# Group B's recurrence in a two-layer decoder trunk: own and neighbour products made elementwise and summed by a ones matmul

## The chip, the cores and the metric

The kernel runs on one core of one Trainium2 chip. The metric is the device time of one execution in microseconds (us), the median of several runs. The engines are TensorE (PE; PEld is its weight load), VectorE (DVE), ScalarE (ACT), GpSimd (POOL) and SyncE (SP), which here issues most of the DMAs.

## What is computed

A trunk of one even and one odd layer over x of 512 tokens by 2048. The even layer has a normalisation, one input projection, two groups of heads (A: windowed attention, B: a gated linear recurrence), gates and an output projection. The odd layer has stick-breaking attention. The change is in group B, which the reference computes for 8 heads of 128 in chunks:

```python
def hgrn2_chunkwise(q, logf, k, v):
    ...
    pair = jnp.exp(jnp.minimum(bcum[:, :, :, :, None, :] - bcum[:, :, :, None, :, :], 0.0))
    att = jnp.einsum('bhnik,bhnjk,bhnijk->bhnij', qc, kc, pair)
    att = jnp.where(causal, att, 0.0)
    o_intra = jnp.einsum('bhnij,bhnjv->bhniv', att, vc)
    ...
    o_inter = jnp.einsum('bhnik,bhnkv->bhniv', qc * jnp.exp(bcum), s_prev)
    o = o_intra + o_inter
```

Here q is SiLU of one projection (bq), k and the forget factor f come from another (bf), v from a third (bi), and a fourth (bg) gives the output gate. Token i sees token j (j not after i) by the sum over the 128 channels of q_i, k_j and the product of the forget factors between them.

## The kernel before

**Projections.** Every tile has 128 partitions by 512 columns (channels by tokens, or a block of 128 tokens by 512 channels). Values of float32 are carried as two exact parts, `hi` on ScalarE (L154) and `lo` on VectorE (L155), both made by `split`. `proj_t` makes 128 output channels for all 512 tokens: 16 pieces of the contraction with three 128x512 matmuls each. `proj_n` makes 512 channels by token blocks. Weights come in chunks through SP (L171) into three raw buffers, are split into three hi and three lo buffers, and `take` keeps the work three chunks ahead. A chunk of `proj_t` holds 8 of the 16 pieces.

**Interleaving.** A head's own work is a generator. After every second piece of a projection (6 matmuls) `tick` runs it up to its next `yield`; the number yielded is how many ticks are left out then. So TensorE's order is written by the program: six or more matmuls of a projection, then one step of a head. `later` queues a generator behind at most one other. The other engines' order is set when the program is built, from the order of the code, its priorities (`urgent`) and its dependences, and each engine runs its own list in order.

**Group B.** For each of the 8 heads the loop at the end of the printed code runs `forget(proj_t)` (bf), `decays`, `gate(proj_t)` for q (L266 to L273: VectorE, ScalarE, VectorE), qd = q times f (L688), `gate(proj_t)` for the output gate, and then queues `attn_b`, whose steps run inside the next head's projections. In head 7, before qd, four tiles of y, the heads' outputs that lie in DRAM (`ydr`), are read back (`load_y`, L297) and split, for the output projection that follows.

**attn_b.** It builds the 128x128 blocks of attention between k and q, transposed, in the tile at0. `blocks` makes four float32 matmuls, one for each token block. The first group uses the bare q and is multiplied by the identity (L610): a token with itself. Then come seven levels: level lv takes runs of 2^lv tokens, and pairs each second run's q with the first run's k. Levels 0 to 4 use `blocks` over the whole block and copy the masked places into at0 (copy_predicated, L636); levels 5 and 6 use small matmuls and ScalarE copies (L627). Every level scales q and k in place by factors of the decay (L631, L633). Blocks that lie further apart go into at1 (L641) and at2 (L650, on ScalarE). The o step then multiplies at0, at1 and at2 with v into one bank, squares the result, splits the square (`x_`), sums it over channels with a matmul against the all-ones tile `onr`, and writes y (L675 to `keep_y`, L290). at0, at1 and at2 are tiles of pool x (19 buffers); q, k and the parts of y are in pool u (62); banks of PSUM for the heads are the 4 of pool pa.

Also met by the prediction: L482 is GpSimd's product in group A's attention, L372 its products in the rotary step, L495 transposes on TensorE.

Of the kernel before, what the change touches and what calls it, by code (L numbers as in the profile page):

```python
# [10 lines left out]
F32R = mybir.dt.float32r  # L11
# [3 lines left out]
ALU = mybir.AluOpType  # L15
# [4 lines left out]
P = 128  # L20
D = 2048
S = 512
NC = D // P
NB = S // P
# [67 lines left out]
def trunk(ctx, tc, xt, w, lnT, lbT, gnT, qkn, sink, cs, amask, bmask, eye, cmask, out):  # L92
# [29 lines left out]
    def bank(pool):  # L122
        cnt[0] += 1
        return pool.tile([P, S], F32, tag="b", name=f"b{cnt[0]}")
# [59 lines left out]
    def proj_t(rhs, c_first=0, c_last=NC - 1):  # L184
        ps = bank(pp)
        c = c_first - 1
        while c < c_last:
            hi, lo, c0, n, wd = take()
            for ci in range(n):
                c = c0 + ci  # L190
                a, b = hi[:, ci * P:(ci + 1) * P], lo[:, ci * P:(ci + 1) * P]
                mm(ps, a, rhs[c][0], c == c_first, False)
                mm(ps, a, rhs[c][1], False, False)
                mm(ps, b, rhs[c][0], False, c == c_last)
                if c % 2:
                    tick()
        return ps
# [64 lines left out]
    def gate(ps, bc):  # L262

        g = U()
        with urgent():
            V.tensor_tensor(out=g, in0=ps, in1=bc, op=ALU.mult)  # L266
        t = U()
        A.activation(out=t, in_=g, func=AF.Abs)
        A.activation(out=t, in_=t, func=AF.Exp, scale=-1.0)
        A.activation(out=t, in_=t, func=AF.Ln, bias=1.0)  # L270
        V.scalar_tensor_tensor(out=t, in0=g, scalar=0.0, in1=t, op0=ALU.min, op1=ALU.subtract)
        A.activation(out=t, in_=t, func=AF.Exp)
        V.tensor_tensor(out=g, in0=g, in1=t, op=ALU.mult)  # L273
        return g
# [313 lines left out]
            V.tensor_tensor(out=res[-1], in0=d[:, :, 0], in1=d[:, :, 1], op=ALU.mult)  # L588
        return res

    def attn_b(hd, decs, k, q, qd, g, v):
        dec = decs[7]
        vc = slice((hd % 4) * P, (hd % 4) * P + P)
        at0 = X()
        at1 = X()
        at2 = X()
        b = bank(pa)

        def blocks(b, q):
            for t in range(NB):  # L600
                s = slice(t * P, (t + 1) * P)
                mm(b[:, s], k[:, s], q[:, s], t == 0, True)

        def halves(x, ln_):
            return x.rearrange("p (n z l) -> p n z l", z=2, l=ln_)

        blocks(b, q)
        q = qd
        v4 = lambda x: x.rearrange("p (b q) -> p b q", b=NB)
        V.tensor_tensor(out=v4(at0), in0=v4(b), in1=ident.unsqueeze(1).to_broadcast([P, NB, P]), op=ALU.mult)  # L610
        yield 2
        for lv in range(7):
            ln_ = 1 << lv
            b = bank(pa)
            if lv < 5:
                blocks(b, q)
            else:
                nw = 64 // ln_
                win = b[:ln_, :NB * 64].rearrange("p (b w q) -> p b w q", b=NB, w=nw)
                for t in range(NB):  # L620
                    for w_ in range(nw):
                        c0 = t * P + 2 * ln_ * w_
                        mm(win[:, t, w_], k[:, c0:c0 + ln_], q[:, c0 + ln_:c0 + 2 * ln_], t + w_ == 0, True)
                a4 = v4(at0)
                for w_ in range(nw):
                    r0 = 2 * ln_ * w_
                    A.activation(out=a4[r0:r0 + ln_, :, r0 + ln_:r0 + 2 * ln_], in_=win[:, :, w_], func=AF.Copy)  # L627
            n = S // (2 * ln_)
            d = decs[lv][:, :2 * n].rearrange("p (n z) -> p n z", z=2)
            qh, kh = halves(q, ln_), halves(k, ln_)  # L630
            V.tensor_tensor(out=qh[:, :, 1], in0=qh[:, :, 1],  # L631
                            in1=d[:, :, 0:1].to_broadcast([P, n, ln_]), op=ALU.mult)
            V.tensor_tensor(out=kh[:, :, 0], in0=kh[:, :, 0],  # L633
                            in1=d[:, :, 1:2].to_broadcast([P, n, ln_]), op=ALU.mult)
            if lv < 5:
                V.copy_predicated(out=v4(at0), mask=bm[lv].unsqueeze(1).to_broadcast([P, NB, P]), data=v4(b))  # L636
            yield 1
        b = bank(pa)
        for i, t in enumerate((1, 3)):
            mm(b[:, i * P:(i + 1) * P], k[:, (t - 1) * P:t * P], q[:, t * P:(t + 1) * P], i == 0, True)  # L640
        A.activation(out=at1[:, :2 * P], in_=b[:, :2 * P], func=AF.Copy)  # L641
        for t in (1, 3):
            qs, ks = q[:, t * P:(t + 1) * P], k[:, (t - 1) * P:t * P]
            V.tensor_scalar(out=qs, in0=qs, scalar1=dec[:, t - 1:t], scalar2=None, op0=ALU.mult)
            V.tensor_scalar(out=ks, in0=ks, scalar1=dec[:, t:t + 1], scalar2=None, op0=ALU.mult)
        yield 1
        b = bank(pa)
        for t in range(2):
            mm(b[:, t * 2 * P:(t + 1) * 2 * P], k[:, t * P:(t + 1) * P], q[:, 2 * P:], t == 0, True)
        A.activation(out=at2, in_=b, func=AF.Copy)  # L650
        yield 1
        o = bank(pa)
        vt = [v[t][:, vc] for t in range(NB)]
        for t in range(NB):
            s = slice(t * P, (t + 1) * P)
            mm(o[:, s], vt[t], at0[:, s], t == 0, False)
        for i, t in enumerate((1, 3)):
            mm(o[:, t * P:(t + 1) * P], vt[t - 1], at1[:, i * P:(i + 1) * P], False, False)
        for t in range(2):
            mm(o[:, 2 * P:], vt[t], at2[:, t * 2 * P:(t + 1) * 2 * P], False, t == 1)  # L660
        sq = X()
        A.activation(out=sq, in_=o, func=AF.Square)
        sh = X(F32R)
        sl = X(F32R)
        split(sq, sh, sl)
        yield 2
        b = bank(pa)
        mm(b, onr, sh, True, False)
        mm(b, onr, sl, False, True)
        vv = X()  # L670
        A.activation(out=vv, in_=b, func=AF.Identity, scale=1.0 / P, bias=epst)
        r = X()
        rsqrt(vv, r, sq)
        y = X()
        V.scalar_tensor_tensor(out=y, in0=o, scalar=gn, in1=r, op0=ALU.mult, op1=ALU.mult)  # L675
        V.tensor_tensor(out=y, in0=y, in1=g, op=ALU.mult)
        keep_y(8 + hd, y)

    for grp in range(2):
        v = evac_nat(proj_n(h, pp, 512), nat0, 512)  # L680
        for hd in range(4 * grp, 4 * grp + 4):
            f, k = forget(proj_t(h), hd)
            decs = decays(f)
            q = gate(proj_t(h), bc0)
            if hd == B_HEADS - 1:
                yy = [load_y(c) for c in range(4)]
            qd = U()
            V.tensor_tensor(out=qd, in0=q, in1=f, op=ALU.mult)  # L688
            g = gate(proj_t(h), bc0)
            later(attn_b(hd, decs, k, q, qd, g, v))  # L690


    def out_proj(cut, resid, finish, yy):
# [232 lines left out]
```

## Time and profile before

| | |
|---|---|
| median of 3 runs | 1831.55 us (1831.22 to 1833.01) |
| profiled execution | 1832.02 us |
| its span | 1830.2 us |
| busy in the span | TensorE 1815.9, its weight loads 1517.9, VectorE 1006.9, ScalarE 775.0, GpSimd 113.2 us |
| DMA | 193.50 MB, mean 106 GB/s |
| stretch of group B's heads | about 363 to 735 us |

The span runs from the first to the last instruction of the profile; the execution's own time has 1.8 us around it. Busy times are those of an engine's instructions; matmuls are pipelined, so one matmul row is longer (0.39 us) than the distance from its start to the next one's. For what a matmul costs, starts are compared.

### The profile page before, as it was taken

The page shows a single profiled execution, that of the slowest core. Times are in us where ns is not written, and L with a number is a line of the kernel's source. Part 1 is how long each engine was busy: PE and PEld are TensorE (multiplying, and loading weights), DVE is VectorE, ACT ScalarE, POOL GpSimd, SP SyncE. Part 2 cuts the span into 40 slices and gives each one's busy share as a digit, 9 for nine tenths or more (in the row PEclk, how much of TensorE's full clock was granted, in tenths as well). Part 3 has the DMA queues.
Part 4 walks back from the last instruction along what each step waited for, and adds up shares of the span by engine and source line. Part 5 has one row for each costly group of instructions (what it writes and reads, how often), then busy time and mean ns, then how long its engine had stood idle before and what let it go on. Part 6 is the DMA issues. An engine that isn't in the chain of part 4 may idle for free.

```text
span 1830.2 us, 22453 instructions
## 1 busy us (share of the span) xinstructions
PE 1815.9 (99%) x8788; PEld 1517.9 (83%) x8788; DVE 1006.9 (55%) x1519; ACT 775.0 (42%) x1285; POOL 113.2 (6%) x96
## 2 busy tenths in 40 slices
PE   8999999999999999999999999999999999999999
PEld 6978888888888888888888888888888888888887
DVE  7486777866456666444435552565355634556334
ACT  6454646544343444334334432544244434444211
POOL 4112212200000000013000000000000000000000
PEclk9999999999999999999999999999999999999999
DMA  6222232222222226334222222222222222235424
GB/s 229 93 83 81 93 104 81 92 81 75 76 86 87 75 98 210 125 137 144 100 92 98 87 92 102 89 87 96 92 89 94 85 99 93 97 115 183 152 81 155
DMA packets 66633, 193.50 MB, mean 106 GB/s; under 512 B 7904, under 2 KB 8416, under 8 KB 66528
## 3 DMA queue, kind: packets, MB, share of 16 engines
q1 hardware_dynamic: 64224, 187.88, 30.2%
q10 hardware_dynamic: 2304, 4.20, 0.7%
q8 instruction: 69, 1.13, 0.2%
q14 instruction: 36, 0.29, 0.0%
HBM read 175.27 MB, written 16.78 MB: 105 GB/s over the span
## 4 chain that ended last, share of the span: by engine, by line
PE 86%; POOL 0%; issue 0%; DVE 0%
PE b L151 85%; PE b L802 1%; PE b L495 0%; POOL x L372 0%; PE b L426 0%; DVE lo L155 0%; DVE u L724 0%; PE b L409 0%; DVE u L374 0%
## 5 line engine op out<-in xcount | busy, mean ns | idle before, releaser
L151 PE MATMUL b<-u,hi 128*128 128x512 f32 x3584 | 1119.8, 394 | 0.0
L151 PEld LDWEIGHTS b<-u,hi 128*128 128x128 f32 x3584 | 663.6, 188 | 131.8
L151 PE MATMUL b<-u,lo 128*128 128x512 f32 x1792 | 699.3, 390 | 0.6 <-DVE lo L155 0.6
L154 ACT ACTIVATE hi<-raw 128x1024 fp32r<-128x1024 f32 (+2 forms) x307 | 312.4, 1018 | 791.9 <-PE b L151 727.0
L155 DVE TENSOR_TENSOR lo<-raw,hi 128x1024 fp32r<-128x1024 f32 (+2 forms) x307 | 363.2, 1184 | 360.8 <-ACT hi L154 353.4
L151 PEld LDWEIGHTS b<-u,lo 128*128 128x128 f32 x1792 | 336.5, 188 | 72.1 <-DVE lo L155 1.0
L151 PE MATMUL b<-hi,u 128*128 128x512 f32 (+1 forms) x1152 | 344.8, 383 | 9.3 <-ACT u L321 6.2
L151 PEld LDWEIGHTS b<-hi,u 128*128 128x128 f32 x1152 | 211.4, 190 | 49.4 <-ACT u L321 6.2
L151 PE MATMUL b<-lo,u 128*128 128x512 f32 (+1 forms) x576 | 218.8, 380 | 0.8 <-DVE lo L155 0.8
L151 PEld LDWEIGHTS b<-u,u 128*128 128x128 f32 (+2 forms) x928 | 115.7, 176 | 14.9 <-issue 3.5
L151 PEld LDWEIGHTS b<-lo,u 128*128 128x128 f32 x576 | 109.2, 190 | 21.5 <-DVE lo L155 1.2
L151 PE MATMUL b<-u,u 128*128 128x128 f32 (+5 forms) x928 | 126.8, 281 | 0.0
L282 POOL TENSOR_TENSOR u<-u,u 128x512 f32<-128x512 f32 x30 | 52.5, 1751 | 523.6 <-ACT u L281 523.0
L266 DVE TENSOR_TENSOR u<-b,bc 128x512 f32<-128x512 f32 x40 | 27.5, 689 | 80.0 <-PE b L151 79.8
L151 PE MATMUL b<-x,u 128*128 128x128 f32 (+3 forms) x360 | 65.4, 327 | 0.0
L155 DVE TENSOR_TENSOR x<-x,x 128x512 fp32r<-128x512 f32 (+2 forms) x56 | 32.4, 578 | 58.4 <-ACT x L154 58.4
L151 PEld LDWEIGHTS b<-x,u 128*128 128x128 f32 x360 | 56.6, 189 | 6.3
L155 DVE TENSOR_TENSOR u<-u,u 128x512 fp32r<-128x512 f32 (+1 forms) x78 | 52.4, 679 | 17.0 <-ACT u L154 17.0
L724 DVE TENSOR_TENSOR u<-b,u 128x512 f32<-128x512 f32 x32 | 22.1, 691 | 65.9 <-PE b L151 65.9
L154 ACT ACTIVATE u<-u 128x512 fp32r<-128x512 f32 (+1 forms) x78 | 47.6, 617 | 22.4 <-DMA u<-ydr 20.2
L701 DVE TENSOR_TENSOR u<-b,u 128x512 f32<-128x512 f32 x32 | 22.0, 690 | 57.8 <-PE b L151 57.8
L787 DVE TENSOR_TENSOR_SCAN x<-one,x 128x512 f32<-128x512 f32 (+1 forms) x64 | 51.0, 818 | 1.6
(145 smaller groups left out, 1125.6 us busy)
## 6 DMA issues: line engine op xcount, KB each, us to landing
raw<-in_w SPq DMA_DIRECT2D x265, 512.0 KB, 3.2
raw<-in_w SPq DMA_DIRECT2D x24, 384.0 KB, 3.0
ydr<-x SPq DMA_DIRECT2D x32, 256.0 KB, 2.6
u<-ydr SPq DMA_DIRECT2D x32, 256.0 KB, 3.7
raw<-in_w SPq DMA_DIRECT2D x18, 256.0 KB, 2.7
u<-in_xt ACTq DMA_DIRECT2D x16, 256.0 KB, 4.8
u<-in_xt SPq DMA_DIRECT2D x16, 256.0 KB, 5.4
x<-u SPq DMA_DIRECT2D x16, 256.0 KB, 2.0
```

The costliest lines, as they stand in the source:

```text
L151: T.matmul(o, l, r, start=start, stop=stop, skip_group_check=True)
L154: A.activation(out=hi, in_=src, func=AF.Copy)
L155: V.tensor_tensor(out=lo, in0=src, in1=hi.bitcast(F32), op=ALU.subtract)
L266: V.tensor_tensor(out=g, in0=ps, in1=bc, op=ALU.mult)
L282: G.tensor_tensor(out=acc, in0=acc, in1=s, op=ALU.add)
L701: V.tensor_tensor(out=r, in0=ps, in1=r, op=ALU.add)
L724: V.tensor_tensor(out=part[n], in0=ps, in1=part[n], op=ALU.add)
L787: V.tensor_tensor_scan(out=r[:, back], data0=one5[:, :e - c], data1=t[:, back], initial=0.0, op0=ALU.mult, op1=ALU.add)
L802: T.transpose(out=o[:, (qb - kb) * P:(qb - kb + 1) * P], in_=zs[qb][:, kb * P:(kb + 1) * P], identity=ident)
```

## The change

- `own_products` is new. Right after qd, ahead of the projection of the output gate, GpSimd multiplies q by k (p0, 128x512, L600 of the changed file) and, at every second token, qd by the k before it (p1, 128x256, L604). Both are split in two parts, p0 into two u tiles, p1 into the halves of one.
- In `attn_b` four ones matmuls (p0's hi and lo, 128x512; p1's, 128x256) take the place of the first `blocks`; they sum over channels and leave each sum in every partition. The product with the identity (L634) places p0's sums in at0, and a masked copy of the odd columns (L637) places p1's.
- Level 0 has no `blocks`, no bank, no masked copy and no `yield` of its own any more; its two scalings (L659, L661) stay.
- The masked copies of levels 1 to 4 (L666) go over the second half of each pair of runs only: 256 of 512 columns.
- Each head's generator has one `yield` less, and what follows level 0 comes earlier by as many ticks.

```diff
--- before.py
+++ after.py
@@ -588,13 +588,31 @@
             V.tensor_tensor(out=res[-1], in0=d[:, :, 0], in1=d[:, :, 1], op=ALU.mult)
         return res
 
-    def attn_b(hd, decs, k, q, qd, g, v):
+    H = S // 2
+
+    def own_products(q, qd, k):
+
+
+        def every_other(x, z):
+            return x.rearrange("p (n z) -> p n z", z=2)[:, :, z]
+
+        p0 = X()
+        G.tensor_tensor(out=p0, in0=q, in1=k, op=ALU.mult)
+        h0, l0 = U(F32R), U(F32R)
+        split(p0, h0, l0)
+        p1 = X()[:, :H]
+        G.tensor_tensor(out=p1, in0=every_other(qd, 1), in1=every_other(k, 0), op=ALU.mult)
+        x1 = U(F32R)
+        h1, l1 = x1[:, :H], x1[:, H:]
+        split(p1, h1, l1)
+        return h0, l0, h1, l1
+
+    def attn_b(hd, decs, k, q, qd, g, v, prods):
         dec = decs[7]
         vc = slice((hd % 4) * P, (hd % 4) * P + P)
         at0 = X()
         at1 = X()
         at2 = X()
-        b = bank(pa)
 
         def blocks(b, q):
             for t in range(NB):
@@ -604,17 +622,27 @@
         def halves(x, ln_):
             return x.rearrange("p (n z l) -> p n z l", z=2, l=ln_)
 
-        blocks(b, q)
+        h0, l0, h1, l1 = prods
         q = qd
         v4 = lambda x: x.rearrange("p (b q) -> p b q", b=NB)
+        b = bank(pa)
+        mm(b, onr, h0, True, False)
+        mm(b, onr, l0, False, True)
+        b1 = bank(pa)
+        mm(b1[:, :H], onr, h1, True, False)
+        mm(b1[:, :H], onr, l1, False, True)
         V.tensor_tensor(out=v4(at0), in0=v4(b), in1=ident.unsqueeze(1).to_broadcast([P, NB, P]), op=ALU.mult)
+        odd = v4(at0).rearrange("p b (n z) -> p b n z", z=2)[:, :, :, 1]
+        m0 = bm[0].rearrange("p (n z) -> p n z", z=2)[:, :, 1]
+        V.copy_predicated(out=odd, mask=m0.unsqueeze(1).to_broadcast([P, NB, P // 2]),
+                          data=b1[:, :H].rearrange("p (b n) -> p b n", b=NB))
         yield 2
         for lv in range(7):
             ln_ = 1 << lv
-            b = bank(pa)
-            if lv < 5:
+            b = bank(pa) if lv else None
+            if 0 < lv < 5:
                 blocks(b, q)
-            else:
+            elif lv:
                 nw = 64 // ln_
                 win = b[:ln_, :NB * 64].rearrange("p (b w q) -> p b w q", b=NB, w=nw)
                 for t in range(NB):
@@ -632,9 +660,12 @@
                             in1=d[:, :, 0:1].to_broadcast([P, n, ln_]), op=ALU.mult)
             V.tensor_tensor(out=kh[:, :, 0], in0=kh[:, :, 0],
                             in1=d[:, :, 1:2].to_broadcast([P, n, ln_]), op=ALU.mult)
-            if lv < 5:
-                V.copy_predicated(out=v4(at0), mask=bm[lv].unsqueeze(1).to_broadcast([P, NB, P]), data=v4(b))
-            yield 1
+            if 0 < lv < 5:
+                m = bm[lv].rearrange("p (n z l) -> p n z l", z=2, l=ln_)[:, :, 1]
+                o4, b4 = (x.rearrange("p (b n z l) -> p b n z l", b=NB, z=2, l=ln_)[:, :, :, 1] for x in (at0, b))
+                V.copy_predicated(out=o4, mask=m.unsqueeze(1).to_broadcast([P, NB, P // (2 * ln_), ln_]), data=b4)
+            if lv:
+                yield 1
         b = bank(pa)
         for i, t in enumerate((1, 3)):
             mm(b[:, i * P:(i + 1) * P], k[:, (t - 1) * P:t * P], q[:, t * P:(t + 1) * P], i == 0, True)
@@ -686,8 +717,9 @@
                 yy = [load_y(c) for c in range(4)]
             qd = U()
             V.tensor_tensor(out=qd, in0=q, in1=f, op=ALU.mult)
+            prods = own_products(q, qd, k)
             g = gate(proj_t(h), bc0)
-            later(attn_b(hd, decs, k, q, qd, g, v))
+            later(attn_b(hd, decs, k, q, qd, g, v, prods))
 
 
     def out_proj(cut, resid, finish, yy):
```

What that does to the engines' lists shows at three places. In the rows below, numbers at the end of names tell tiles apart, and "waits" names whose work an instruction waits for (DMAHW is a DMA).

TensorE, in the projection bf of head 1 (b_3470, now b_3492), where head 0's generator takes its first step. Before:

```order
L151 MATMUL b_3470<-u_100,hi_3300 128x512
L151 MATMUL b_3470<-u_101,hi_3300 128x512
L151 MATMUL b_3470<-u_100,lo_3301 128x512
L151 MATMUL b_3486<-u_2899,u_2749 128x128 [waits PE_49]
L151 MATMUL b_3486<-u_2899,u_2749 128x128 x3
L151 MATMUL b_3470<-u_153,hi_3300 128x512
L151 MATMUL b_3470<-u_154,hi_3300 128x512
L151 MATMUL b_3470<-u_153,lo_3301 128x512
```

Now:

```order
L151 MATMUL b_3492<-u_100,hi_3322 128x512
L151 MATMUL b_3492<-u_101,hi_3322 128x512
L151 MATMUL b_3492<-u_100,lo_3323 128x512
L151 MATMUL b_3508<-u_2912,onr 128x512 [waits PE_49]
L151 MATMUL b_3508<-u_2913,onr 128x512
L151 MATMUL b_3511<-u_2918,onr 128x256 [waits PE_49]
L151 MATMUL b_3511<-u_2918,onr 128x256
L151 MATMUL b_3492<-u_153,hi_3322 128x512
L151 MATMUL b_3492<-u_154,hi_3322 128x512
L151 MATMUL b_3492<-u_153,lo_3323 128x512
```

The first step stands at the same place; four float32 matmuls of 128x128 have become four with `onr`, two of them half as wide.

VectorE, in the gate projection of head 1, where group A's second half still runs. u_3307 (before: u_3296) is qd, u_3312 the lo part of p0, the L155 rows that read a bank (b_) make lo parts of group A's probabilities out of PSUM. Before:

```order
L273 TENSOR_TENSOR u_3287<-u_3287,u_3289 128x512 [waits Activation_49]
L520 TENSOR_TENSOR x_3338<-b_3335,x_3338 64x256 [waits Activation_49]
L688 TENSOR_TENSOR u_3296<-u_3287,u_3197 128x512 [waits DVE_49]
L520 TENSOR_TENSOR x_3338<-b_3335,x_3338 64x256 [waits Activation_49]
L522 TENSOR_TENSOR x_3270<-x_3338,u_2067 128x128 [waits DVE_49]
L522 TENSOR_TENSOR x_3271<-x_3338,u_2229 128x128
L155 TENSOR_TENSOR lo_3377<-raw_3375,hi_3376 128x1024 [waits DMAHW2_49,PE_49,Activation_49]
L155 TENSOR_TENSOR x_3363<-b_3357,x_3362 128x512 [waits DMAHW7_49,Activation_49]
L155 TENSOR_TENSOR x_3372<-b_3366,x_3371 128x512 [waits Activation_49,Pool_49]
```

Now:

```order
L273 TENSOR_TENSOR u_3298<-u_3298,u_3300 128x512 [waits Activation_49]
L719 TENSOR_TENSOR u_3307<-u_3298,u_3208 128x512 [waits DVE_49]
L659 TENSOR_TENSOR u_3307<-u_3307,u_3208 128x256 [waits Pool_49]
L155 TENSOR_TENSOR u_3312<-x_3309,u_3311 128x512 [waits Activation_49]
L155 TENSOR_TENSOR x_3339<-b_3333,x_3338 128x512 [waits Activation_49]
L155 TENSOR_TENSOR u_3317<-x_3315,u_3317 128x256 [waits Activation_49]
L155 TENSOR_TENSOR x_3348<-b_3342,x_3347 128x512 [waits Activation_49]
L155 TENSOR_TENSOR lo_3399<-raw_3397,hi_3398 128x1024 [waits DMAHW2_49,PE_49,Activation_49]
```

Between qd and the splits of group A now stand a scaling that waits for GpSimd and the split of p0; p1's split stands between those of group A. The bank b_3333 is free, for the transposes that TensorE makes next, when x_3339 is written.

ScalarE, in the gate projection of head 7. The hi tile (before hi_5796, now hi_5875) belongs to weights; u_5730, u_5736, u_5742 (now u_5795, u_5801, u_5807) are the hi parts of the second to fourth tile of y; L650 (now L681) is at2 of head 6, L662 (now L693) the square of its o. Before:

```order
L154 ACTIVATE hi_5796<-raw_5795 128x1024 [waits DMAHW6_49,PE_49]
L154 ACTIVATE u_5730<-u_5728 128x512 [waits DMAHW2_49]
L641 ACTIVATE x_5535<-b_5787 128x256 [waits PE_49]
L650 ACTIVATE x_5536<-b_5813 128x512 [waits PE_49]
L154 ACTIVATE u_5736<-u_5734 128x512 [waits DMAHW3_49]
L154 ACTIVATE hi_5884<-raw_5883 128x1024 [waits DMAHW7_49,PE_49]
L154 ACTIVATE u_5742<-u_5740 128x512 [waits DMAHW5_49]
L662 ACTIVATE x_5838<-b_5829 128x512 [waits PE_49]
```

Now:

```order
L154 ACTIVATE hi_5875<-raw_5874 128x1024 [waits DMAHW6_49,PE_49]
L154 ACTIVATE u_5795<-u_5793 128x512 [waits DMAHW2_49]
L154 ACTIVATE u_5801<-u_5799 128x512 [waits DMAHW3_49]
L154 ACTIVATE u_5807<-u_5805 128x512 [waits DMAHW5_49]
L154 ACTIVATE u_5815<-x_5813 128x512 [waits Pool_49]
L681 ACTIVATE x_5577<-b_5843 128x512
L154 ACTIVATE u_5821<-x_5819 128x256 [waits Pool_49]
L693 ACTIVATE x_5868<-b_5859 128x512 [waits PE_49]
```

at2 stood ahead of the third and fourth tile of y; now it stands behind all four and behind p0's split.

SP, the same place, now (u_5793, u_5799, u_5805 are the second to fourth tile of y; raw_6055 goes into the buffer of raw_5874, which hi_5875 and its lo part read):

```order
L171 DMA raw_6009<-in_w 128x1024 [waits DMAHW5_49,DVE_49]
L297 DMA u_5793<-ydr 128x512
L297 DMA u_5799<-ydr 128x512 [waits PE_49,Pool_49]
L171 DMA raw_6055<-in_w 128x1024 [waits DMAHW6_49,DMAHW4_49,DVE_49]
L297 DMA u_5805<-ydr 128x512
L297 DMA u_5930<-ydr 128x512 [waits PE_49]
```

The read of the fourth tile stands behind the load of raw_6055, as it stood behind such a load before.

## Rows read from the trace of the kernel before

**Rows 1.** The page, busy time, share and instructions of each engine.

```profile
PE 1815.9 (99%) x8788; PEld 1517.9 (83%) x8788; DVE 1006.9 (55%) x1519; ACT 775.0 (42%) x1285; POOL 113.2 (6%) x96
```

**Rows 2.** Chain that ended last, in order of time: start, length, what.

```profile
365.49 604.57 PE b L151 x3060
```

**Rows 3.** Timeline of TensorE: start, length, instructions.

```profile
60.00 0.40 PE L151 MATMUL b<-hi,u 128*128 128x256 f32 x2
60.24 0.28 PE L151 MATMUL b<-lo,u 128*128 128x256 f32 x1
...
599.79 0.64 PE L151 MATMUL b<-x,onr 128*128 128x512 f32 x2
600.27 0.63 PE L151 MATMUL b<-u,hi 128*128 128x512 f32 x2
...
601.66 1.06 PE L151 MATMUL b<-u,u 128*128 128x128 f32 x8
...
603.93 0.62 PE L151 MATMUL b<-u,hi 128*128 128x512 f32 x2
...
606.65 1.05 PE L151 MATMUL b<-u,u 128*128 128x128 f32 x8
```

**Rows 4.** Groups by line and shape, 363 to 735 us; GpSimd's L482, all its instructions.

```profile
L636 DVE COPY_PREDICATED x<-u,b 128x512 f32<-128x512 int32 x40 | 29.6, 741 | 0.0
L631 DVE TENSOR_TENSOR u<-u,u 128x256 f32<-128x256 f32 x56 | 23.7, 422 | 24.9 <-PE b L151 24.9
...
L482 POOL TENSOR_TENSOR x<-x,dn 128x512 f32<-128x512 f32 x24 | 33.2, 1408 | 0.0
L482 POOL TENSOR_TENSOR x<-x,dn 128x256 f32<-128x256 f32 x8 | 5.8, 724 | 159.1 <-DVE dn L480 80.2 <-ACT hi L154 72.6 <-ACT u L268 3.7
...
L482 POOL TENSOR_TENSOR x<-x,dn x32: 613/1040/2112, 145.3 to 347.7; 128x512 f32<-128x512 f32 x24, 128x256 f32<-128x256 f32 x8
```

**Rows 5.** Timelines of TensorE and VectorE at the q gate of head 5.

```profile
582.86 0.39 PE L151 MATMUL b<-u,lo 128*128 128x512 f32 x1
...
583.28 0.69 DVE L266 TENSOR_TENSOR u<-b,bc 128x512 f32<-128x512 f32 x1 [2.18 <-PE b L151]
...
587.85 0.68 DVE L273 TENSOR_TENSOR u<-u,u 128x512 f32<-128x512 f32 x1
```

**Rows 6.** Timelines of ScalarE and SP, head 7's gate projection.

```profile
677.14 1.06 ACT L154 ACTIVATE hi<-raw 128x1024 fp32r<-128x1024 f32 x1 [1.99 <-PE b L151]
678.11 0.62 ACT L154 ACTIVATE u<-u 128x512 fp32r<-128x512 f32 x1
...
681.41 0.60 ACT L650 ACTIVATE x<-b 128x512 f32<-128x512 f32 x1 [2.42 <-PE b L151]
...
679.62 0.33 SPq L171 DMA_DIRECT2D raw<-in_w  x1
680.00 0.43 SPq L297 DMA_DIRECT2D u<-ydr  x1
```

**Rows 7.** DMA issues: queue, count, KB each, median us from issue to landing.

```profile
u<-ydr SPq DMA_DIRECT2D x32, 256.0 KB, 3.7
...
x<-u SPq DMA_DIRECT2D x16, 256.0 KB, 2.0
```

**Rows 8.** Windows: length, busy of PE, PEld, DVE, ACT, POOL; granted clock, DMA share, GB/s.

```profile
6.20:12.60 6.40, 6.36 (x14) 4.70 (x15) 3.58 (x6) 4.01 (x6) 1.79 (x1) 1.00 0.84 263
1826.50:1828.50 2.00, 0.00 (x0) 0.00 (x0) 0.69 (x1) 0.00 (x0) 0.00 (x0) 1.00 0.21 79
1828.50:1830.20 1.70, 0.00 (x0) 0.00 (x0) 0.00 (x0) 0.00 (x0) 0.00 (x0) 0.51 0.17 61
```

**Rows 9.** Timelines of VectorE and TensorE, the last stop of TensorE; brackets: idle before.

```profile
249.90 1.23 DVE L273 TENSOR_TENSOR u<-u,u 128x512 f32<-128x512 f32 x1
251.76 0.69 DVE L374 TENSOR_TENSOR u<-u,u 128x512 f32<-128x512 f32 x1 [0.64 <-POOL x L372]
...
253.64 0.51 PE L151 MATMUL b<-lo,u 128*128 128x512 f32 x1 [0.80 <-DVE lo L155]
```

## The prediction, made before the changed kernel ran

> **What bounds the kernel now.** I read the head of the page first, for the engines' shares [rows 1]: TensorE is busy 99% of the span, VectorE 55%, ScalarE 42%, GpSimd 6%. Then I read the chain that ended last in order of time [rows 2]: its piece that begins at 365.49 is 604.57 us of matmuls without a break. L151 is the helper through which every projection and every head records. The eight heads of group B run inside that piece, up to 735 us, so today TensorE waits there for nobody. Two things alone can change the time: what TensorE itself executes, and a wait that doesn't exist now. Work that VectorE loses is worth nothing, and work that GpSimd gains costs nothing, unless its place in an engine's order makes TensorE wait.
>
> The sum is made against the profiled execution, 1832.02 us; the median of the runs is 1831.55, 0.47 less, which I take off at the end. About 0.2% (3.66 us) is what a measurement of this kernel can tell from no change.
>
> **What TensorE saves.** Per head two groups of `blocks` go (own products and level 0), and a pair of 128x512 and a pair of 128x256 ones matmuls come. One group of `blocks` is the row of 8 instructions; between two such rows lie 4.99 us with 18 matmuls of a projection, whose pitch is 0.2267 (12 of them in the 2.72 us between 603.93 and 606.65) [rows 3]. So a group costs 4.99 - 4.08 = 0.91 us, 0.23 for each 128x128 matmul in it. A pair with the ones matrix takes 0.48 (599.79 to 600.27), a pair of 128x256 of the same type 0.24 (60.00 to 60.24, in an early projection). For one more change of operands I add 0.03. Per head 2 x 0.91 - 0.75 = 1.07, for eight heads **-8.6 us** (8.0 if the change costs 0.10; 8.8 if it costs nothing).
>
> **What costs nothing by itself.** Five masked copies a head at 0.74 us become five at half the width; the nearest row at 128x256 is 0.42 [rows 4]. Two more splits a head on VectorE and ScalarE come. Cover: TensorE's 99%. The distance between two levels stays 12 projection matmuls, 2.72 us, and a level's two scalings and copy (three at 0.42) are shorter than before (1.58). If a half-width copy still cost 0.74, nothing would follow from it.
>
> **GpSimd's new products are not free where they stand.** p0 is a 128x512 product, p1 a 128x256 one with a stride. The nearest rows are the products of L482: 1.41 us mean at 128x512, 0.72 at 128x256, and all of them together run from 0.61 to 2.11 with a median of 1.04 [rows 4]. I take 1.5 and 0.75, near the means; 1.04 and 0.61 are the low ends, 2.1 and, by the same stretch, 1.2 the high ones. Per head they run after the q gate, whose pace head 5 shows [rows 5]: the projection's last matmul starts at 582.86, so TensorE goes on at 583.09; L266 starts at 583.28 (0.2 later) and L273 ends at 588.53, 5.25 after that. With 5.2, L273 ends 5.4 us after the projection, p0 at 6.9, p1 at 7.65.
>
> What waits behind them, each engine being in order:
> - VectorE's level-0 scaling L659 (it rewrites what p1 reads) and p0's lo split now stand ahead of group A's splits (the VectorE excerpt). The scaling (0.42) ends at 8.0, the split (0.69, with the same overlap of 0.08 between operations that runs through this part) at 8.65, the next at 9.3. In head 1 that last one frees the bank that TensorE's transposes need after 26 projection matmuls and 12 transposes, 5.9 + 12 x 0.11 = 7.2 us: **+2.1** (1.4 to 3.1). In head 0 the second such split comes after p1's too, at 10.25, and is needed after 9.3: **+1.0** (0.2 to 2.0).
> - ScalarE's split of p0 now stands ahead of the previous head's copy at2 (L650 of before, L681 of after), because that head's steps come two ticks earlier. The copy ends at 6.9 + 0.62 + 0.60 less the overlap: 8.05. TensorE needs it after 8.14 us in heads 2, 5 and 6 (24 projection matmuls, 8 of 128x128 at 0.23, two of 128x256 at 0.44): 0.15 each for the spread of p0, **+0.4** (0 to 1.6). In head 3 it needs it after 6.33: **+1.7** (1.2 to 2.3). Head 4's window is 12 us: nothing.
> - Head 7 is the dear one, and it isn't GpSimd's. There four reads of y (`load_y`) are issued inside, and on ScalarE the at2 copy now stands behind the splits of all four (the ScalarE excerpt); before, it stood ahead of the last two. The fourth read is issued on SP behind a weight load that waits for a split of weights, whose buffer TensorE frees with the last matmuls ahead of the o step, and it is this step that needs the at2 copy. Today the same links read [rows 6]: ScalarE's hi split starts at 677.14, the weight load goes out at 679.62 and y at 680.00, 2.86 us in all, with the lo split between; today's at2 copy, at 681.41, waits for TensorE only. A read of y lands after 3.7 us [rows 7]; then come three ScalarE operations, y's split, p0's split and the copy, 0.54 + 0.54 + 0.60. That is 8.24 us from the start of the hi split, and TensorE's own work until it needs the copy is one matmul and six of 128x128, done 1.35 after that start. **+6.9** (5.2 with a landing of 2.0, the shortest in the table of issues; 8.6 with the same step the other way).
>
> **The clock.** TensorE stops nowhere for that long now. The nearest rows are the two ends of the program [rows 8]: in the 2 us behind the last matmul the granted clock still reads 1.00, and in the stretch after that 0.51, so it fell to the lower of its levels about 2 us into idleness. At the start, after 6.24 us without work, 14 matmuls take 6.4 us (the clock column reads 1.00 there, but the pace is half): at 0.2267 they would take 3.2. A stop of 6.9 us in head 7 resembles the start most, so **+3.2** (0 to 3.2). The stops in heads 0 to 6 are about 2 us at most, and I let them cost their own length.
>
> Sum: -8.6 + 2.1 + 1.0 + 0.4 + 1.7 + 6.9 + 3.2 = **+6.7**, so 1838.7 for the profiled execution and **1838.2** beside the median.
>
> **A rule against this change.** GpSimd and VectorE hold each other up here already [rows 9]: VectorE's L273, 0.68 us elsewhere, takes 1.23 at 249.90 beside a product of GpSimd, the next VectorE product then waits 0.64 for GpSimd, and TensorE stands 0.80 ahead of 253.64 for the weight split behind it. It's the same chain that I expect in heads 0 and 1. The Trainium skill, "SBUF — State Buffer", section "SBUF: two separate sides", has the pair of ports that these two engines share as an exclusive lock: of a VectorE instruction with two SBUF inputs and a GpSimd one that reads SBUF, whichever starts first has it for its whole length. The stretched L273 agrees with it. In this change p0 and L719 become ready at the same moment. Without any such effect p0 takes 1.04 and p1 0.61: heads 0 and 1 then lose 0.4 and 1.5, heads 2, 5, 6 nothing, head 3 1.25, and the sum is +4.6. With one VectorE product (0.69) wholly ahead, p0 ends 1.73 after the gate and p1 0.72 later, and the sum is +7.9. My 1.5 and 0.75 lie between.
>
> **Rivals.**
> 1. The clock stays up through head 7's stop: +3.5, so 1835.1. For it: the fall seen is after the last matmul, where nothing follows. Against: the start shows that pace returns late. 0.20.
> 2. GpSimd's waits are hidden, head 7's stands: -8.6 + 10.1 = +1.5, 1833.1. For it: nothing is missing in heads 2, 5, 6 with p0 at 1.4. Against: heads 1 and 3 lack over 1 us even at 1.04 and 0.61. 0.06.
> 3. GpSimd slow, p0 2.1 and p1 1.2: the chains behind it are 0.6 to 1.05 longer, heads 0 to 6 lose 9.0 in place of 5.2, and head 1's stop of 3.1 brings the clock down once more, +3.2: +13.7, 1845.3. 0.07.
> 4. The other side, faster: ScalarE's at2 copy in head 7 is not held. Its place is that one copy; its price is 6.9 + 3.2. With GpSimd's waits as I have them -8.6 + 5.2 = -3.4, 1828.2; with p0 and p1 at their low ends (3.2) -5.4, 1826.1, faster. It decides only where the hold falls below 1 us or so and the clock stays; since landing is 3.7 of the 8.24, even a read that landed at once would leave 3.2, so the fourth read would have to go out before TensorE frees that buffer. For it: the weight load ahead of it is all that delays it, and SP is idle most of the time. Against: the order on SP. 0.10.
> 5. As 4, and all of GpSimd's waits hidden too: -8.6, 1823.0. 0.05.
>
> **How the numbers follow.** The forecast has the rest, 0.52. Faster (below 1827.9) takes 5 and half of 4, 0.10; same (to 1835.2) takes 2, half of 1, the other half of 4 and the forecast's lowest edge, 0.28; slower 0.62. The forecast alone spans 1835 to 1842. The range goes down to 1828.5 to take in 1 and 2 and leaves out 4, 5 (0.15) and 3 (0.07), about 2 in 10: 1828.5 to 1842.5.
>
> **What would show it.** Right: in the chain in order of time the piece of 604.57 us is cut in head 7's third projection, by the ScalarE copy L681 behind y's split, with TensorE idle 5 to 8 us and a granted clock below 1.00 behind it; smaller cuts in heads 0, 1 and 3, released by VectorE L155 and ScalarE L681 with GpSimd L600 or L604 behind them. Wrong: no gap of over 2 us near 680 us, then 4 or 5; a gap without a fall of the clock, then 1; as many us of matmuls in heads 0 to 6 as before, then the first term fails.

## The result, and the profile after

The changed kernel takes 1845.68 us (median of 6 runs, 1844.51 to 1848.34) against 1831.65 (6 runs): ratio 1.0077, 95% interval 1.0067 to 1.0087, so 14.0 us slower. The forecast was slower, by 6.7 us. The profiled execution took 1847.46, and 0.85 of its 15.5 us more in span arise in the first 30 us, where the program is the same in both.

The head of the page after, which answers to [rows 1]:

```profile
span 1845.7 us, 22296 instructions
PE 1815.4 (98%) x8692; PEld 1511.5 (82%) x8692; DVE 1007.3 (55%) x1535; ACT 783.2 (42%) x1301; POOL 132.9 (7%) x112
```

TensorE is busy as long as before, although it has less to do: part of that time ran at half pace. Whom TensorE waited for after 253 us, in the view of waits (total us, times, longest):

```profile
PE b L151 <- ACT x L681: 8.4, 2, 6.8
PE b L495 <- DVE x L155: 5.3, 1, 5.3
PE b L151 <- DVE x L155: 1.0, 2, 0.8
PE b L151 <- DVE lo L155: 0.8, 1, 0.8
PE b L151 <- DVE u L661: 0.5, 1, 0.5
```

Before, only the one of 0.8 was there [rows 9]. TensorE's timeline gives the places: the matmul that ended each wait, with the idle time ahead of it in brackets. By place they are: the gate projections of heads 0 and 1; head 3's gate projection, where an earlier head's steps run; head 2's levels; and head 7's gate projection.

```profile
322.85 0.73 PE L151 MATMUL b<-x,u 128*128 128x512 f32 x2 [0.82 <-DVE x L155]
323.78 0.50 PE L151 MATMUL b<-x,u 128*128 128x512 f32 x1 [0.20 <-DVE x L155]
...
367.16 1.11 PE L495 MATMUL b<-ident,x 128*128 128x128 f32 x4 [5.29 <-DVE x L155]
...
458.44 1.13 PE L151 MATMUL b<-x,u 128*128 128x256 f32 x4 [1.55 <-ACT x L681]
...
474.51 1.13 PE L151 MATMUL b<-u,u 128*128 128x128 f32 x8 [0.50 <-DVE u L661]
...
693.20 2.07 PE L151 MATMUL b<-x,u 128*128 128x256 f32 x4 [6.82 <-ACT x L681]
```

The clock, windows with the columns of [rows 8]:

```profile
366.00:370.00 4.00, 2.84 (x9) 2.46 (x10) 3.89 (x8) 2.36 (x6) 0.00 (x0) 0.50 0.00 0
372.00:374.00 2.00, 2.00 (x10) 1.65 (x9) 1.06 (x3) 0.76 (x2) 0.00 (x0) 1.00 0.00 0
...
686.40:688.50 2.10, 0.00 (x0) 0.00 (x0) 1.97 (x3) 0.99 (x2) 0.00 (x0) 1.00 0.18 31
688.50:693.20 4.70, 0.00 (x1) 0.01 (x1) 1.03 (x2) 1.63 (x3) 0.00 (x0) 0.55 0.59 209
693.20:699.40 6.20, 6.20 (x15) 4.92 (x16) 2.66 (x6) 1.64 (x3) 1.17 (x1) 0.51 0.00 0
699.40:701.00 1.60, 1.60 (x9) 1.30 (x8) 0.00 (x0) 0.00 (x0) 0.00 (x0) 1.00 0.00 0
```

In head 7 TensorE stops at about 686.4. The granted clock reads 1.00 up to 688.5 and 0.55 in the rest of the stop, so it falls there to the lower level (1.2 of 2.4 GHz), and after the work goes on it stays there for 6.2 us. Behind the stop in head 1 the same happens, and the upper level is back by 372.

Since TensorE's list is known, the start of the same matmul in both traces gives what each stretch lost, bracketed idle time and half pace together:

| stretch | us lost | forecast |
|---|---|---|
| first 30 us, same program | 0.85 | - |
| head 0's wait (320.76 to 321.67 before, 321.61 to 324.12 now) | 1.6 | 1.0 |
| head 1: the stop, by starts | 5.7 | 2.1 |
| head 1: half pace behind it | 2.1 | 0 |
| at2 copies behind heads 2, 5, 6's p0 (o step to its sum 6.62, elsewhere 6.34) | 0.8 | 0.4 |
| the same behind head 3's p0 (8.15) | 1.8 | 1.7 |
| levels 1 and 2 waiting for scalings, above all head 2 | 1.0 | 0 |
| head 7: the stop, by starts | 7.0 | 6.9 |
| head 7: half pace behind it | 2.9 | 3.2 |
| saved by TensorE, 8 heads | -8.6 | -8.6 |
| sum | 15.2 of 15.5 | 6.7 |

The saving is as forecast: a quiet head's period, 43.90 us before (568.84 to 612.74 at L565), is 43.11 now with a wait of 0.28 in it, so 1.07 a head. And head 7's chain is link for link the one of [rows 6]. The changed kernel's chain in that stretch, in order of time:

```profile
684.85 1.07 ACT hi L154
...
685.94 1.24 DVE lo L155
...
687.20 0.33 SPq L171
...
687.58 3.91 DMA u<-ydr
...
691.51 1.15 ACT u L154 x2
692.66 0.49 ACT x L681
```

### The profile page after: what moved, and what is told of

It is laid out like the page before. It is cut to its first block, busy times and chain, and to the rows that moved or that the text cites. A ratio compares the mean times of both kernels' runs of the same rounds, so it can differ in the third digit from the quotient of the medians.

```text
span 1845.7 us, 22296 instructions
## 1 busy us (share of the span) xinstructions
PE 1815.4 (98%) x8692; PEld 1511.5 (82%) x8692; DVE 1007.3 (55%) x1535; ACT 783.2 (42%) x1301; POOL 132.9 (7%) x112
## 4 chain that ended last, share of the span: by engine, by line
PE 82%; DVE 2%; ACT 1%; issue 1%; POOL 0%; DMA 0%; SPq 0%; POOLq 0%; ACTq 0%
PE b L151 81%; PE b L834 1%; DVE lo L155 0%; ACT x L477 0%; POOL x L372 0%; PE b L495 0%; DMA u<-ydr 0%; ACT hi L154 0%; POOL x L600 0%; DVE u L271 0%; ACT u L272 0%; DVE x L458 0%; DVE x L520 0%; DVE mx L461 0%; DVE u L273 0%
## 5 line engine op out<-in xcount | busy, mean ns | idle before, releaser
L155 DVE TENSOR_TENSOR lo<-raw,hi 128x1024 fp32r<-128x1024 f32 (+2 forms) x307 | 363.5, 1185 | 356.4 <-ACT hi L154 353.7
L151 PEld LDWEIGHTS b<-u,u 128*128 128x128 f32 (+2 forms) x800 | 98.6, 173 | 15.0 <-issue 4.4
L151 PE MATMUL b<-u,u 128*128 128x128 f32 (+5 forms) x800 | 110.1, 282 | 0.5 <-DVE u L661 0.5
L266 DVE TENSOR_TENSOR u<-b,bc 128x512 f32<-128x512 f32 x40 | 27.5, 689 | 95.5 <-PE b L151 95.4
L155 DVE TENSOR_TENSOR u<-u,u 128x512 fp32r<-128x512 f32 (+1 forms) x78 | 52.3, 679 | 19.5 <-ACT u L154 19.5
L155 DVE TENSOR_TENSOR x<-x,x 128x512 fp32r<-128x512 f32 (+2 forms) x56 | 32.4, 578 | 31.5 <-ACT x L154 31.5
```

The costliest lines, as they stand in the source:

```text
L151: T.matmul(o, l, r, start=start, stop=stop, skip_group_check=True)
L155: V.tensor_tensor(out=lo, in0=src, in1=hi.bitcast(F32), op=ALU.subtract)
```

## The experiments

Theory A: the changed kernel loses what it saves because of where its instructions stand in the lists of ScalarE and VectorE; in head 7 the at2 copy stands behind a read of y, in heads 0 and 1 group A's splits stand behind GpSimd's products and the late q gate. The rivals are named with the runs. All results are medians, the ratio is that of the runs to those of before on the same chip. The kernel before read 1831.65 beside the result and 1832.1 to 1832.3 beside these runs, so a difference from the changed kernel's 1845.68 is good to about half a us.

**One head's products later.** In three runs `own_products` of one head alone is called behind the gate projection (here head 7; the others with 1 and 0):

```diff
-            prods = own_products(q, qd, k)
+            prods = None if hd == 7 else own_products(q, qd, k)
             g = gate(proj_t(h), bc0)
+            prods = prods or own_products(q, qd, k)
```

Head 7. 

> The changed kernel, with own_products of head 7 alone called after the gate projection. ScalarE's at2 copy then stands ahead of the splits of y and of p0 there. Theory A (that copy's place is what stops TensorE in head 7): the stop of 6.8 us near 686 us and the half-pace clock behind it (3.0) both go, 9.9 together: 1845.7 - 9.9 = 1835.8 (1834.5 to 1837). Rival B (the fourth read of y itself is late, whoever stands behind it): a stop of the same size turns up where TensorE reads y, at the start of the output projection: above 1842. All other stops (heads 0, 1, 3) stay as they are.

Measured: 1846.11 us, ratio 1.0078 (1.0062 to 1.0093): no gain. A's number fails. B's (above 1842) is met, but not for B's reason: no stop shows in the output projection. TensorE's stop behind L681 in head 7 is gone, as A says, but TensorE now waits for the products themselves, in its timeline of this run:

```profile
699.15 0.80 PE L151 MATMUL b<-u,onr 128*128 128x512 f32 x1 [5.70 <-ACT u L154]
700.56 0.79 PE L151 MATMUL b<-u,onr 128*128 128x512 f32 x1 [0.61 <-DVE u L155]
```

The clock falls here as well (0.50 from 701 to 703 us). Heads 4 to 7 take their first step right behind their own gate projection, so here the products are needed early. In heads 0 to 3 the first step comes 40 to 50 us behind it: head 0's, placed in head 1's bf further up, stands in head 2's, at 380.19. In heads 0 and 1 TensorE therefore doesn't miss products that come later. I hadn't looked at who waits for a product that comes late. The run shows that the at2 copy was held by its place; it doesn't show what mending that is worth.

Head 1. 

> The changed kernel, with own_products of head 1 alone called after the gate projection, so that group A's splits stand ahead of what waits for GpSimd. Theory A (products ahead of the splits, on top of a VectorE that is late there): the stop of 5.3 us at 361.9 and its clock fall (2.2 at half pace) go: 1845.7 - 7.7 = 1838.0 (1837 to 1839.5). Rival C (VectorE is late at this place anyway, L266 starts some 3.5 us behind TensorE in the changed kernel and 2 in the one before): a stop of 3 us or more stays in head 1, 1841 to 1843.

Measured: 1840.56, ratio 1.0046 (1.0029 to 1.0063), 5.1 below the changed kernel by the medians, outside A's span by 1 and just below C's. The spans of the two profiled executions differ by 7.7 (1845.7 and 1838.0), which is A's number. The profile decides: TensorE's wait at that place is 0.5 in place of 5.3, and no fall of the clock lies there; head 7's 6.6 and the others stay. VectorE's L266 is as late as in the changed kernel (357.61, 3.8 behind the projection for q). So place, not lateness alone, made that stop. C fails by the stop, A by the size of the total.

Head 0. 

> The changed kernel, with own_products of head 0 alone called after the gate projection. Head 0's stop (1.0 by the rows, 1.6 with the starts compared) goes. Theory F (VectorE's lateness ahead of head 1's q gate is partly head 0's doing: 3.5 us here, 2.0 in the kernel before): head 1's stop falls from 5.3 to about 3.8: 1845.7 - 1.6 - 1.5 = 1842.6. Rival G (that lateness is made by head 1's own forget gate and group A): the stop stays at 5.3 and the time is 1844.1.

Measured: 1844.32, ratio 1.0063 (1.0046 to 1.0079), which is G's number. Of the waits of TensorE in the list after 253 us, these two are left, and the 0.8 and 0.5 at its end:

```profile
PE b L151 <- ACT x L681: 8.2, 2, 6.6
PE b L495 <- DVE x L155: 5.4, 1, 5.4
```

Head 0's wait is gone and head 1's is as long as it was. VectorE's lateness there isn't inherited from head 0's products.

**Three tiles of y in head 7.**

```diff
-                yy = [load_y(c) for c in range(4)]
+                yy = [load_y(c) for c in range(3)]
```

> The changed kernel, with three of the four tiles of y read inside head 7 (the fourth with the others at the start of the output projection). ScalarE's at2 copy then stands behind a weight split, two splits of y that have landed and p0's split. Theory A (the wait for the fourth read is what the copy stands behind): what is left of head 7's stop is 1.06 + 0.54 + 0.54 + 0.54 + 0.60 - 1.35 = 1.9 us and the clock stays up: 1845.7 - 5.0 - 3.0 = 1837.7 (1836.5 to 1839). Rival E (p0's split, waiting for GpSimd, holds the copy): no change, 1845.7. If the fourth tile is late in the output projection, a new stop of up to 3 us is added there.

Measured: 1838.17, ratio 1.0038 (1.0025 to 1.0051), as A has it. Head 7's stop, in TensorE's timeline of this run, is now

```profile
686.74 1.13 PE L151 MATMUL b<-x,u 128*128 128x256 f32 x4 [1.62 <-ACT x L681]
```

(1.9 by starts), the granted clock stays 1.00 behind it, and no new stop shows in the output projection. The read of the fourth tile was what the copy stood behind. E falls: p0's split is still ahead of the copy.

**Products on VectorE.**

```diff
-        G.tensor_tensor(out=p0, in0=q, in1=k, op=ALU.mult)
+        V.tensor_tensor(out=p0, in0=q, in1=k, op=ALU.mult)
...
-        G.tensor_tensor(out=p1, in0=every_other(qd, 1), in1=every_other(k, 0), op=ALU.mult)
+        V.tensor_tensor(out=p1, in0=every_other(qd, 1), in1=every_other(k, 0), op=ALU.mult)
```

> The changed kernel, with p0 and p1 made on VectorE instead of GpSimd, at the same place in the code. Theory A (GpSimd's slower products are the smaller part, the order is the larger): from L273 to the split that head 1 waits for, 4.3 us become 3.2; heads 0 and 1 lose 1.1 less each, head 3 1.0 less, heads 2, 5, 6 0.8 less together; head 7 stays: 1845.7 - 4.0 = 1841.7 (1840 to 1843.5). Rival D (GpSimd, slow and blocking VectorE, is the whole cause in heads 0 to 6): all their stops go, about 12 us: 1833 to 1835.

Measured: 1840.66, ratio 1.0048 (1.0033 to 1.0063), in A's span and far from D's. Head 1's stop is still 3.74 in TensorE's timeline of this run:

```profile
363.14 1.12 PE L495 MATMUL b<-ident,x 128*128 128x128 f32 x4 [3.74 <-DVE x L155]
```

And the clock still falls, in its windows (columns of [rows 8]):

```profile
362.00:364.00 2.00, 0.85 (x5) 0.86 (x5) 1.97 (x6) 2.00 (x4) 0.00 (x0) 0.78 0.00 0
364.00:366.00 2.00, 2.00 (x7) 1.61 (x6) 2.00 (x4) 0.47 (x2) 0.00 (x0) 0.50 0.00 0
```

From L273's end to the end of the split that TensorE waits for are 2.7 us (360.36 to 363.08), with GpSimd 4.3. Two things differ there: the products are faster, and VectorE's list has changed. Group A's split (first row) now stands ahead of p0's (in the second row), not behind it:

```profile
362.40 0.68 DVE L155 TENSOR_TENSOR x<-b,x 128x512 fp32r<-128x512 f32 x1
363.00 1.02 DVE L155 TENSOR_TENSOR u<-x,u 128x512 fp32r<-128x512 f32 x2
```

That place is worth 0.6 of the 1.6 us. Heads 2, 3, 5 and 6 lose nothing, for a reason that I hadn't counted: in this build ScalarE's list has the at2 copy ahead of p0's split again (449.86 and 452.05 us). So GpSimd's price is some 1.0 us in head 1, about the 1.1 that A gave it; for the copies this run can't separate speed from order.

**Half-width copies alone**, in the kernel before: the masked copies of levels 0 to 4 as in the change, nothing else.

```diff
-                V.copy_predicated(out=v4(at0), mask=bm[lv].unsqueeze(1).to_broadcast([P, NB, P]), data=v4(b))
+                m = bm[lv].rearrange("p (n z l) -> p n z l", z=2, l=ln_)[:, :, 1]
+                o4, b4 = (x.rearrange("p (b n z l) -> p b n z l", b=NB, z=2, l=ln_)[:, :, :, 1] for x in (at0, b))
+                V.copy_predicated(out=o4, mask=m.unsqueeze(1).to_broadcast([P, NB, P // (2 * ln_), ln_]), data=b4)
```

> The kernel before, with only the masked copies of levels 0 to 4 made over the half that the mask can hold. Theory: TensorE sets the time and a copy ends well ahead of the next level, so nothing follows: within 0.3 us of before. Rival: VectorE, which is late in heads 0 and 1, gains there: 0.8 us or more below, if TensorE's one stop of 0.8 at 253 us goes, which lies ahead of the first copy, so hardly. A copy at 128x256 takes 0.42 us if it goes as other operations of that size, 0.74 if by the mask's steps.

Measured: 1831.66 against 1832.18, ratio 0.9999 (0.9989 to 1.0008): no difference that these runs can tell, as expected. A copy takes 0.55 us on average, between the two guesses, where [rows 4] had 0.74; the group by line in this run:

```profile
L638 DVE COPY_PREDICATED x<-u,b 128x256 f32<-128x256 int32 x40 | 21.9, 549 | 0.0
```

**The steps two ticks later.** Level 0 yields again:

```diff
-            if lv:
-                yield 1
+            yield 1
```

> The changed kernel, with level 0's yield given back (it does no matmul there, but the steps behind it come two ticks later, as in the kernel before). Theory A (the at2 copies are late because the steps come earlier): head 3's stop of 1.8 falls to 0.3, the 0.3 each of heads 2, 5, 6 go, and in head 7 TensorE asks for the copy a weight piece later, so that about 2 of 7 us are left and the clock stays up: 1845.7 - 1.5 - 0.8 - 5.0 - 2.5 = 1835.9 (1834 to 1839). Heads 0 and 1 stay as they are (9.4 with the clock). Rival: the place in ScalarE's list alone decides, however late TensorE asks: 1843 or more.

Measured: 1835.28, ratio 1.0016 (1.0007 to 1.0026): 10.4 us below the changed kernel by one line, as A expects. The waits of TensorE:

```profile
PE b L495 <- DVE x L155: 5.3, 1, 5.3
PE b L151 <- ACT x L671: 1.3, 1, 1.3
PE b L151 <- DVE x L155: 1.3, 3, 0.8
PE b L151 <- DVE lo L155: 0.8, 1, 0.8
```

This file is one line shorter, so its L680 is the at2 copy and its L671 that of at1 (L672 in the changed kernel). No wait for at2 is left in any head, and none for level 1's scaling (L661). In head 7 ScalarE's list now has both copies behind the splits of y and of p0, at 689.75 and 690.01; TensorE asks for at1 10.8 us behind the q gate's L272, where it asked for at2 4.4 us behind it in the changed kernel, and 1.3 us are left. The rival falls.

**The parts together.** `own_products` behind the gate projection in heads 0 and 1, three tiles of y in head 7:

> The changed kernel with two of its places mended at once: own_products called after the gate projection in heads 0 and 1, three tiles of y in head 7; products on GpSimd. What is left by the theory: of head 1 0.5, heads 2, 5, 6 0.8 together, head 3 1.8, level 0's scalings 0.8, head 7 1.9, against 8.8 saved: 1831.7 - 3.0 = 1828.7 (1827 to 1830.5). If the stops are not separate (one mended makes the next longer), 1832 or more.

Measured: 1831.45, ratio 0.9996 (0.9987 to 1.0006). It misses by 2.8 us. Half a us of that is the kernel before, 1832.18 on this chip and not 1831.7, and the profiled execution (1830.87) is another 0.6 below the median. In it, by starts, heads 0 and 1 lose 1.15 and not 0.5, the at2 copies and the scalings 3.6 and not 3.4, head 7 the 1.9 that was expected, and 8.6 and not 8.8 are saved; about half a microsecond I can't place.

With the products on VectorE as well:

> As the run before it, and p0 and p1 on VectorE. Heads 2, 3, 5 and 6 lose nothing then (as with the products on VectorE alone): 1831.7 - 8.8 + 0.5 + 0.8 + 1.9 = 1826.1 (1824.5 to 1828). Rival: VectorE's 1.1 us more a head make it late elsewhere in heads 0 and 1: 1829 or more.

Measured: 1827.93, ratio 0.9977 (0.9968 to 0.9987), inside the span. With two tiles of y:

> As the run before it, with two tiles of y read inside head 7. ScalarE's at2 copy stands behind one split less: 0.5 below the run before it (1825.6). If the tiles read later are missed by TensorE at the start of the output projection, a new stop of 1 to 4 us there and the total above the run before it.

Measured: 1827.61, ratio 0.9974 (0.9964 to 0.9985): the two can't be told apart. In the profile the stop in head 7 is 1.1 in place of 2.1, and one of 0.3 comes up in the output projection, at 710.58.

Level 0's yield given back, and the products later in heads 0 and 1:

> The changed kernel with level 0's yield given back and own_products called after the gate projection in heads 0 and 1; products on GpSimd, four reads of y. What the runs so far leave: 1.2 in heads 0 and 1, 1.8 in head 7, 0.3 elsewhere, against 8.6 saved: 1832.0 - 8.6 + 3.3 = 1826.7 (1825.5 to 1828.5), faster than both kernels. If the parts don't add up, up to 1831.

Measured: 1827.15, ratio 0.9971 (0.9960 to 0.9983). With the products on VectorE:

> As the run before it, with p0 and p1 on VectorE. Heads 0 and 1 lose 0.4 in place of 1.2: 1826.0 (1825 to 1828). Rival: with the steps two ticks later GpSimd's time is covered, and nothing changes: 1826.7.

Measured: 1826.21, ratio 0.9968 (0.9955 to 0.9980). TensorE's waits in that run:

```profile
PE b L151 <- ACT x L671: 1.3, 1, 1.3
PE b L151 <- DVE lo L155: 0.8, 1, 0.8
```

The 1.3 is again head 7's at1 copy. Both beat both kernels, by 5 to 6 us against before. The intervals of the two overlap: with the steps later, what GpSimd's slowness costs is below what these runs can tell.

## Why the prediction was right in sign and wrong in size

- TensorE's saving, the masked copies at no price, head 3's and head 7's waits, the fall of the clock in head 7: right, within 0.3 us each. Three tiles of y and level 0's yield confirm the mechanism that was named for head 7 and the at2 copies, the copy's place and the two ticks.
- **The step that failed is "L266 starts at 583.28 (0.2 later)" [rows 5]**, head 5's pace of the q gate taken for heads 0 and 1. In head 1 VectorE is late when that gate begins. The projection for q ends at 354.23 in the changed kernel (its last matmul starts at 354.00), and L266 starts at 358.01, 3.8 later. The timelines of TensorE (first row) and VectorE:

```profile
354.00 0.39 PE L151 MATMUL b<-u,lo 128*128 128x512 f32 x1
...
358.01 0.68 DVE L266 TENSOR_TENSOR u<-b,bc 128x512 f32<-128x512 f32 x1
...
362.10 0.69 DVE L273 TENSOR_TENSOR u<-u,u 128x512 f32<-128x512 f32 x1 [0.70 <-ACT u L272]
362.83 0.69 DVE L719 TENSOR_TENSOR u<-u,u 128x512 f32<-128x512 f32 x1
365.47 0.43 DVE L659 TENSOR_TENSOR u<-u,u 128x256 f32<-128x256 f32 x1 [1.95 <-POOL x L604]
365.81 0.68 DVE L155 TENSOR_TENSOR u<-x,u 128x512 fp32r<-128x512 f32 x1
366.42 0.68 DVE L155 TENSOR_TENSOR x<-b,x 128x512 fp32r<-128x512 f32 x1
```

  From L266's start to the end of the last row are 9.1 us; the forecast had 9.1 from 0.2 after the projection. So the chain has the length that was forecast and was put 3.6 us too early, and 2.1 + 3.6 is the 5.7 measured. That the lengths agree is in part luck: the gate took 4.8 and not 5.25 up to L273's end, and from there to L659's start, behind both products, are 2.7 and not 2.25. The kernel before would have told: there the projection's last matmul starts at 351.53 and VectorE's L266 only at 354.04, 2.3 after its end (the same two timelines of before):

```profile
351.53 0.39 PE L151 MATMUL b<-u,lo 128*128 128x512 f32 x1
...
345.03 1.79 DVE L155 TENSOR_TENSOR lo<-raw,hi 128x1024 fp32r<-128x1024 f32 x1 [1.07 <-ACT hi L154]
346.75 1.52 DVE L570 SCALAR_TENSOR_TENSOR u<-u,u 128x512 f32<-128x512 f32 x1
348.30 1.41 DVE L571 TENSOR_TENSOR u<-u,u 128x512 f32<-128x512 f32 x1
...
354.04 0.68 DVE L266 TENSOR_TENSOR u<-b,bc 128x512 f32<-128x512 f32 x1
```

  VectorE has no pause from 345.03 to that L266: it makes head 1's own forget gate and decays (L570 to L588), two weight splits and one split of group A. Its first three operations, shown above, are long ones: group A's products on GpSimd (L482, 344.13 to 349.17) run beside them, and in head 5, where none do, the same three take 1.23, 0.68 and 0.69. The difference, 2.1 us as an estimate from these rows, is nearly the whole 2.3; no run moves L482, so that it is the cause is not shown. The prediction had named such a hold-up [rows 9], but counted it only for the change's own products. Nothing was waiting for the lateness then.

  What makes the other 1.5 of the 3.8 is open. It is there ahead of those three rows, which are as long in the changed kernel (1.80, 1.53, 1.41): the first starts at 348.98 there, 3.95 later, where TensorE is 2.47 later. The change's products on GpSimd are not it: L266 starts 3.7 behind the projection with head 0's products late (351.77 to 355.44) and with all products on VectorE (351.87 to 355.58).
- **The clock in head 1 follows from that step.** A stop of 2.1 was let off; one of 5.3 cost 2.1 more at half pace. Rival 3 had a second fall of the clock there, for another reason (slow GpSimd), and 1845.3, close to the result; but p0 took 1.66 us and p1 0.89 on average, nearer the middle values (1.5, 0.75) than the high ones (2.1, 1.2), in the groups by line of the changed kernel (columns of [rows 4]):

```profile
L600 POOL TENSOR_TENSOR x<-u,u 128x512 f32<-128x512 f32 x8 | 13.3, 1663 | 335.1 <-DVE u L273 234.5 <-PE b L151 100.6
L604 POOL TENSOR_TENSOR x<-u,u 128x256 f32<-128x256 f32 x8 | 7.1, 886 | 8.8 <-issue 8.8
```

- Smaller terms: head 0 (1.6 for 1.0) has the same kind of chain; the at2 copies of heads 2, 5, 6 cost 0.28 each for 0.15. The levels' scalings (1.0) were set to nothing because 2.72 us lie between levels; VectorE's other work in that stretch was not looked at. Level 0's yield takes that wait away.
- The range ended at 1842.5, because the one rival above it was given 0.07.
- The rule of the Trainium skill, "SBUF — State Buffer", section "SBUF: two separate sides", a lock between VectorE and GpSimd, is borne out in part. Where p0 and L719 become ready together, in heads 0 to 6, p0 takes 1.68 to 1.75, close to the 1.73 that was worked out for it. But in head 7, at 683.47, VectorE stands still beside it and it takes 1.29, not 1.04, so the hold-up is nearer 0.4 than a whole VectorE operation (0.69). For the change's own products it is the smaller part: with both on VectorE head 1 still stops for 3.7 of 5.3 us.

## What to carry to other kernels

Where one engine is busy all the time, a change that shortens its own work is decided by who else's list it reorders: for each instruction that is put ahead of another, compare when the later one is ready with when the bound engine asks for it, in that very stretch, since an engine that is idle in one head is late in another. Making an interleaved piece of work shorter moves all its later steps earlier, and a copy that was in time may then stand behind a DMA; giving back an empty step cost nothing and saved 10 us here. A stop of the bound engine that brings its clock down is paid a second time at half pace (2.1 and 2.9 us here).

## What the runs showed of the hardware that I had not expected

- The price of a stop isn't its length. Stops of 1.3 to 2.1 us left the granted clock at 1.00 (in the run with three tiles of y, products on VectorE and heads 0 and 1 mended, a stop of 2.14 at 676.56 did); one of 3.7 was followed by half pace for 3.4 us (to about 366.6), one of 5.3 for 4.3 (to about 371.5), one of 6.8 for 6.2 us. The Trainium skill, "TensorE: Matmul & The Clock Gate", section "What's actually happening", says that the throttled state is the default and that activity releases it; the rows agree, since the lower level stays on after the work has begun again.
- That price may differ from run to run. The five runs with three tiles of y lie at 1838.1 to 1838.2 (three) and 1840.3 to 1840.6 (two), and the one that was profiled has one fall of the clock, in head 1; the kernel before, which has none, lay within 1.1 us in its eight runs on that chip. The granted clock, as a mean over the run, was 0.998 or 0.999 in the former and 0.997 in the latter. That head 1's fall makes the difference, and which price a run gets, is not shown here.
- A masked copy's price follows its layout and not only its size. At 128x256 the level copies take 0.50 us on average: 0.42 to 0.43 at levels 2 to 4, where runs of 4 to 16 columns are copied, and 0.72 at level 1, with runs of 2 (in head 4: 573.10 for level 1, 575.62, 580.36 and 584.13 for the others). The one of single odd columns (L637) takes 0.73, as much as the full width took before. The groups of the changed kernel:

```profile
L666 DVE COPY_PREDICATED x<-u,b 128x256 f32<-128x256 int32 x32 | 16.0, 501 | 0.0
L637 DVE COPY_PREDICATED x<-u,b 128x256 f32<-128x256 int32 x8 | 5.8, 726 | 0.0
```
